# An RWKV-7 scan's tokens to token-major form by two transpositions and two full products, one sums' corner in another bank, thirteen low parts on GpSimd

## The chip, the cores and the metric

The kernel runs on one core of one Trainium2 chip. The metric is the time of one execution in device microseconds; lower is better. One execution of the kernel before was also taken by the hardware profiler, and all rows below are of that one. PE is the matmul engine (TensorE) and PEld its weight load, DVE is VectorE, ACT ScalarE, POOL GpSimd, SP the engine that issues the DMAs.

## The reference

A hybrid decoder of two layers over 272 tokens (16 learned meta tokens and 256 inputs) of width 2048: layer 0 mixes by RWKV-7, layer 1 by stick-breaking attention, each followed by a SwiGLU network. The change touches layer 0's mixing alone, whose core is a scan with 32 heads of 64:

```python
kk = heads(k * k_k)
kk = kk * lax.rsqrt(jnp.maximum(jnp.sum(kk * kk, axis=-1, keepdims=True), 1e-24))
k = k * (1.0 + (a - 1.0) * k_a)
def step(state, inp):
    r_t, d_t, k_t, v_t, kk_t, a_t = inp
    sa = jnp.einsum('bhvk,bhk->bhv', state, -kk_t)
    state = (state * d_t[:, :, None, :]
             + sa[..., None] * (kk_t * a_t)[:, :, None, :]
             + v_t[..., None] * k_t[:, :, None, :])
    return state, jnp.einsum('bhvk,bhk->bhv', state, r_t)
...
mean = jnp.mean(y, axis=-1, keepdims=True)
var = jnp.mean(jnp.square(y - mean), axis=-1, keepdims=True)
y = ((y - mean) * lax.rsqrt(var + GN_EPS)).reshape(b, l, d) * gn_w + gn_b
bonus = (jnp.sum(rh * kh * r_k, axis=-1, keepdims=True) * vh).reshape(b, l, d)
out = ((y + bonus).astype(h.dtype) * g) @ w_o
```

## The kernel before

**Numbers and layout.** Activations lie with the feature on the partitions and the token on the free axis. A product of full precision is three matmuls of a short float form: high part by high part, low by high, high by low (`mm3k`, L205 to L207). A high part is a cast on ACT, the low part what DVE subtracts (`whl_pair`, L233 and L234, for weights; `parts`, L1218 and L1219, and `split` for activations).

**The scan.** `scan` runs over 16 pairs of heads, one pair to 128 partitions, in a pipeline of several pairs: in round n, pair A = n makes its states and outputs, M = n + 1 the inverse of its triangular blocks, B = n + 2 its scores, and C = n + 3 its decays and keys. Rounds 0 to 12 are steady and come from `period`, which lists the work in the order in which PE executes it; the rounds before and after have an order of their own. Between the pieces, `f(k)` takes k steps from a stream: each step is the three matmuls of one block of 128 rows of the V or R projection of a coming pair, and the stream also splits the weights, a 128x512 piece to every four steps, several pieces ahead of use.

**Order.** PE's order and SP's are as written. On DVE, ACT and POOL the framework's scheduler places the instructions, by what they need and when it thinks that this comes; a few are tied by hand. An engine executes its instructions in order.

**Pieces that the change touches.**
- The eight PSUM banks are given out in steady rounds by `PLAN` (L50): the names in one bank's string take turns in it, and each waits until the one before was read. `ba` and `bb` hold the scores of the two heads, `b00` and `b01` the blocks of `neg` (L1380, one per head), `rm0` and `rm1` the transition products (L1524), `z0` the scores of the 16 meta tokens (L1300), `cb` the states and outputs of pair A.
- `lora` makes a pair's decay (`ld`, `L`, `P`, `Q`) from `zw`, the iclr `ta` from `za`, and keys: `AR0` and `ARV` (scaled queries, keys and values; four chunks by three kinds by 64 tokens), `B0` and `BK` (two kinds). `after_v` and `after_r` fill in the values and queries as the projections come out.
- `turned` and `tokens` bring the chunks into token-major form: `tb` by transposition, `tv` by products with an identity (`ident`, keys) and a centering matrix (`cen`, values), 64 tokens each, four each, and `X` takes both from one 128x512 copy. `values` adds the products `kv`, two copies into `X`; `apply` (L1506) multiplies by the inverse `Tt` and copies the results `Ah` and, into `X`, the states' input.
- The block inverses: `scores` masks `sb` into `G` on DVE (L1351), a DMA brings the blocks to `As`, `solve` on POOL inverts the 16x16 blocks (L1402, L1404), `inverse` brings them back as `Tt` by DMA (L1411, L1414), and `left` and `right` (`yb` L1476, `Ys`, `zb` L1495) double the block size.
- Group norm: `A.sq` is y squared (L1569); `parts` splits it into `hs`; `norm` multiplies `hs` by a block of ones (`vb`, L1213 as in `bonus`) and finishes on ACT and DVE. In `period` the split stands behind `C.lora()`, then come eight stream steps, then `norm`.
- The output projection: the stream's last steps split the pairs' outputs `o` (L953, `split`, DVE at L277) and multiply them. `KHEAD` = 13 outputs are used by the first four blocks.

Of the kernel before, what the change touches and what calls it, by code (L numbers as in the profile page):

```python
# [49 lines left out]
PLAN = {name: bank for bank, names in {  # L50
    "pfr0": "zb32 b00 z0v bonus gp", "pfr1": "wa yb16 zw kv", "psc0": "ba b01 zb16 za",
    "psc1": "bb rm0 tv vb", "psd0": "cb yb32", "psd1": "z0 rm1 tb k0"}.items()
    for name in names.split()}
# [5 lines left out]
ASTEP = 4  # L59
BUFS = {n: 2 for n in "BK AR0 G An Tt X BV0".split()}  # L60
BUFS.update(ARV=3, bv=3, pe=4)

# [75 lines left out]
class Builder:  # L138
# [132 lines left out]

    def split(self, src, pool):

        nc = self.nc
        x = self.pair_tile(pool, src.shape[1])
        nc.scalar.copy(x[0], src)
        nc.vector.tensor_tensor(x[1], src, x[0].bitcast(F32), ALU.subtract)  # L277
        return x
# [103 lines left out]
    def time_mix(self):  # L382
# [15 lines left out]
        with ExitStack() as ctx:  # L398
# [3 lines left out]
            self.s2 = []  # L402
            zero = sp.tile([128, 4, 2, 2, 64], F32, name="zero", tag="X", bufs=BUFS["X"])
            zero = zero.rearrange("p a b c t -> p (a b c t)")[:, :325]
# [381 lines left out]
    def period(self, n, A, M, B, C, D, f):  # L786

        M.inverse()
        if n > 0:
            A.right(32)  # L790
        A.start()
        B.scores(0)
        B.scores(1)
        if n > 0:
            A.apply()
        B.chunk0()
        B.chunk0_out()
# [12 lines left out]
        M.right(16)  # L810
        A.step(4)
        B.tokens(A.copied)
        B.bonus()
        C.lora()
        A.squares = A.parts(A.sq)
        f(8)
        A.norm()
        f(8)
        M.left(32)
        B.values()  # L820
        f(4)
# [103 lines left out]
    def stream(self, pairs):  # L925
# [22 lines left out]
        for m, k in steps:  # L948
# [3 lines left out]
            while len(self.o) <= k:  # L952
                self.o.append(self.split(self.oraw[len(self.o)], self.xs1))  # L953
            self.mm3k(self.wo[m], next(w), self.o[k], k == 0, False)
# [232 lines left out]
class Pair:  # L1187
# [34 lines left out]
    def lora(self):  # L1222
# [34 lines left out]

        self.ARV = ARV = self.big("ARV", 4, 3, 64)
        self.BK = BK = self.big("BK", 4, 2, 64)
# [8 lines left out]
        def par(tile, first, second):  # L1268
# [4 lines left out]
        V.scalar_tensor_tensor(AR0[:, 0], kk[:, :META], -1.0, P[:, :META], ALU.mult, ALU.mult)  # L1273
        V.scalar_tensor_tensor(ARV[:, :, 1], kk[:, META:].rearrange("p (c t) -> p c t", t=C), -1.0,
                               Pc[:, :, :C], ALU.mult, ALU.mult)
# [6 lines left out]
    def after_v(self, vp):  # L1282
        A = self.A
        A.copy(self.V0[:, 32:32 + META], vp[:, :META])
        A.copy(self.ARV[:, :, 2], vp[:, META:].rearrange("p (c t) -> p c t", t=C))

    def after_r(self, rp):
        V = self.V
        V.tensor_tensor(self.AR0[:, 1], rp[:, :META], self.P[:, 1:17], ALU.mult)
        V.tensor_tensor(self.ARV[:, :, 0], rp[:, META:].rearrange("p (c t) -> p c t", t=C),  # L1290
                        self.Pc[:, :, 1:], ALU.mult)
# [3 lines left out]

    def chunk0(self):

        z0 = self.b.rbank("z0")
        for h in HS:
            self.PE.matmul(z0[h, 0:32], self.B0[h], self.AR0[h].rearrange("p s t -> p (s t)"),  # L1300
                           start=True, stop=True)
        self.z0 = z0
# [29 lines left out]
    def scores(self, i):  # L1332
# [4 lines left out]
        for c, h in ORDER[4 * i:4 * i + 4]:  # L1337
            u = (c - 1) * 128
            for s in range(2):
                self.PE.matmul(self.sb[h][HS[s], u:u + 128], self.BK[HS[h], c - 1, s],  # L1340
                               self.ARV[HS[h], c - 1, 0:2].rearrange("p s t -> p (s t)"),
                               start=True, stop=True)
# [32 lines left out]
    def neg(self):  # L1375
        b = self.b
        b0 = [b.rbank("b00"), b.rbank("b01")]
        for c, h in ORDER:
            q, r = (c - 1) // 2, (c - 1) % 2
            self.PE.matmul(b0[h][HS[r], q * 64:(q + 1) * 64], self.ARV[HS[h], c - 1, 1],  # L1380
                           self.BK[HS[h], c - 1, r], start=True, stop=True)
# [4 lines left out]
    def bonus(self):  # L1386
        bp = self.head_sums("bonus", self.b.blk[0], self.rk, 0)
        self.bv = self.t272("bv")
        self.V.tensor_tensor(self.bv[:, :META], self.V0[:, 32:32 + META], bp[:, :META], ALU.mult)
        c4 = lambda x: x[:, META:].rearrange("p (c t) -> p c t", t=C)  # L1390
        self.b.last = self.V.tensor_tensor(c4(self.bv), self.ARV[:, :, 2], c4(bp), ALU.mult)

# [33 lines left out]
    def tokens(self, after=None):  # L1426
# [5 lines left out]
        tv = b.rbank("tv", 1)  # L1432
        for r in range(2):
            for q in range(2):
                u = (r * 2 + q) * 128
                c = q * 2 + r
                PE.matmul(tv[HS[r], u:u + 128], self.ARV[:, c, 1], b.cst("ident"), start=True, stop=True)
                PE.matmul(tv[HS[1 - r], u:u + 128], self.ARV[:, c, 2], b.cst("cen"), start=True, stop=True)
        for r in range(2):
            with b.tc.issue_after(after.ins) if after else nullcontext():  # L1440
                A.copy(self.G0[:, :, :, r],
                       tb[:, r * 256:r * 256 + 256].rearrange("p (q h t) -> p h q t", q=2, h=2))
        self.X = X = self.big("X", 4, 2, 2, 64)
        A.copy(X[:, :, 0], tv.rearrange("p (c h t) -> p c h t", c=4, h=2))

    def values(self):
# [4 lines left out]
        for h in range(2):  # L1451
            for c in range(1, 5):
                q, r = (c - 1) // 2, (c - 1) % 2
                PE.matmul(kv[HS[r], (h * 2 + q) * 64:(h * 2 + q + 1) * 64],
                          self.G2[HS[1 - r], h, q, r], X[HS[1 - r], r * 2 + q, 0, h],
                          start=True, stop=True)
        for h in HS:
            PE.matmul(k0[h, 0:64], self.SC0[h, 0:64], self.BV0[h, 64:128], start=True, stop=True)
        for r in range(2):
            A.copy(X[HS[r], r * 2:r * 2 + 2, 1],  # L1460
                   kv[HS[r], 0:256].rearrange("p (h q t) -> p q h t", q=2, h=2))
        self.KV0 = self.big("KV0", 64)
# [36 lines left out]
    def apply(self):  # L1499
# [3 lines left out]
        for h in range(2):  # L1503
            for c in range(1, 5):
                q, r = (c - 1) // 2, (c - 1) % 2
                self.PE.matmul(wa[HS[r], (h * 2 + q) * 128:(h * 2 + q + 1) * 128],  # L1506
                               self.Tt[HS[r], h * 2 + q], X[HS[r], r * 2 + q, :, h],
                               start=True, stop=True)
# [4 lines left out]
        for r in range(2):  # L1513
            b.latest = self.A.copy(X[HS[r], r * 2:r * 2 + 2, 0], wa4[HS[r], :, :, 1])

    def trans(self):
# [9 lines left out]
        for r in range(2):  # L1526
# [3 lines left out]
            b.last = V.tensor_tensor(self.Rh.rearrange("p (q r) t -> p q r t", q=2)[:, :, r], x[:, :, 1],  # L1530
                            self.ARV.rearrange("p (q r) s t -> p q r s t", q=2)[:, :, r, 0], ALU.add)

# [116 lines left out]
```

## Time and profile before

| | |
|---|---|
| median of 3 runs | 2640.32 us (2638.05 to 2641.45) |
| the profiled execution's own time | 2635.57 us |
| its span | 2633.8 us |
| instructions | 54589 |
| scan, from the first weights' steps to the last | about 165 to 600 us of the span |
| a steady round | 24.54 us |
| granted TensorE clock | 1.00 |

The profiled execution lasts 1.8 us longer than its span, and 4.75 us less than the median of the runs. Starts in the rows are us from the start of the span. Sums of row lengths are no PE time: matmuls overlap, so what counts is the distance from start to start. In rows of waits the name behind the arrow is what came last.

### The profile page before, as it was taken

The page shows a single profiled execution, that of the slowest core. Times are in us where ns is not written, and L with a number is a line of the kernel's source. Part 1 is how long each engine was busy: PE and PEld are TensorE (multiplying, and loading weights), DVE is VectorE, ACT ScalarE, POOL GpSimd, SP SyncE. Part 2 cuts the span into 40 slices and gives each one's busy share as a digit, 9 for nine tenths or more (in the row PEclk, how much of TensorE's full clock was granted, in tenths as well). Part 3 has the DMA queues.
Part 4 walks back from the last instruction along what each step waited for, and adds up shares of the span by engine and source line. Part 5 has one row for each costly group of instructions (what it writes and reads, how often), then busy time and mean ns, then how long its engine had stood idle before and what let it go on. Part 6 is the DMA issues. An engine that isn't in the chain of part 4 may idle for free.

```text
span 2633.8 us, 54589 instructions
## 1 busy us (share of the span) xinstructions
PE 2614.5 (99%) x21238; PEld 2448.2 (93%) x21238; DVE 1787.7 (68%) x3606; ACT 1496.0 (57%) x3049; POOL 182.4 (7%) x493
## 2 busy tenths in 40 slices
PE   9999999999999999999999999999999999999999
PEld 8898999889999999999999999998888888888888
DVE  7677777857555555555558775788766666666665
ACT  7776666756544444444446664786555454554553
POOL 0014445430000000000000000000000000000000
PEclk9999999999999999999999999999999999999999
DMA  6444445445555655655655555434565665665655
GB/s 228 147 122 131 119 112 130 110 131 186 171 171 173 182 171 173 184 171 169 184 171 172 178 169 176 144 113 150 184 190 179 196 190 176 200 186 180 199 181 176
DMA packets 186388, 439.45 MB, mean 167 GB/s; under 512 B 58736, under 2 KB 89616, under 8 KB 186128
## 3 DMA queue, kind: packets, MB, share of 16 engines
q1 hardware_dynamic: 184784, 432.77, 53.3%
q8 instruction: 166, 2.72, 0.4%
q0 software_dynamic: 768, 2.23, 0.3%
q10 hardware_dynamic: 576, 0.96, 0.1%
q14 instruction: 94, 0.77, 0.1%
HBM read 430.15 MB, written 5.74 MB: 165 GB/s over the span
## 4 chain that ended last, share of the span: by engine, by line
PE 96%; DVE 2%; ACT 1%; DMA 1%; POOL 0%; issue 0%; SPq 0%; ACTq 0%; POOLq 0%
PE mm L210 23%; PE mm L205 17%; PE mm L207 17%; PE mm L206 17%; PE mm L209 12%; PE lr L607 1%; PE mm L508 1%; PE cb L1561 1%; DVE G L1351 1%; PE zb L1495 1%; PE z L1145 1%; PE yb L1476 1%; PE cb L1553 0%; DMA Tt<-s 0%; PE ba L1340 0%; PE hms L1060 0%
## 5 line engine op out<-in xcount | busy, mean ns | idle before, releaser
L187 DVE TENSOR_TENSOR wlo<-raw,whi 128x512 fp32r<-128x512 f32 (+1 forms) x1432 | 967.7, 679 | 597.9 <-ACT whi L186 577.8
L186 ACT CAST whi<-raw 128x512 fp32r<-128x512 f32 (+1 forms) x1432 | 870.9, 610 | 837.1 <-PE mm L206 530.5
L205 PE MATMUL mm<-hl,whi 128*128 128x272 f32 x3328 | 961.8, 289 | 0.0
L207 PE MATMUL mm<-hl,wlo 128*128 128x272 f32 x3328 | 960.4, 289 | 0.0
L206 PE MATMUL mm<-hl,whi 128*128 128x272 f32 x3328 | 958.0, 288 | 0.0
L210 PE MATMUL mm<-hl,whi 128*128 128x512 f32 x2624 | 919.9, 394 | 0.0
L209 PE MATMUL mm<-hl,wlo 128*128 128x256 f32 x2624 | 738.5, 282 | 0.1
L206 PEld LDWEIGHTS mm<-hl,whi 128*128 128x128 f32 x3328 | 631.1, 190 | 0.0
L205 PEld LDWEIGHTS mm<-hl,whi 128*128 128x128 f32 x3328 | 625.4, 188 | 3.4 <-issue 1.7
L207 PEld LDWEIGHTS mm<-hl,wlo 128*128 128x128 f32 x3328 | 625.5, 188 | 0.2
L210 PEld LDWEIGHTS mm<-hl,whi 128*128 128x128 f32 x2624 | 492.6, 188 | 111.8
L209 PEld LDWEIGHTS mm<-hl,wlo 128*128 128x128 f32 x2624 | 494.4, 188 | 1.1 <-DVE ht L1067 0.4
L234 DVE TENSOR_TENSOR wlo<-raw,whi 128x512 fp32r<-128x512 f32 (+2 forms) x156 | 105.6, 690 | 20.1 <-ACT whi L233 18.0
L233 ACT CAST whi<-raw 128x512 fp32r<-128x512 f32 (+2 forms) x156 | 91.8, 608 | 23.2 <-PE mm L206 20.8
L1402 POOL TENSOR_TENSOR Tm<-As 40x14 f32<-40x14 f32 (+6 forms) x224 | 85.0, 379 | 211.2 <-DMA As<-s 169.8
L226 DVE TENSOR_TENSOR h<-h,mm 128x256 f32<-128x256 f32 (+1 forms) x224 | 93.9, 420 | 6.7 <-PE mm L210 6.0
L1404 POOL TENSOR_TENSOR As<-As,Tm 40x14 f32<-40x14 f32 (+6 forms) x224 | 86.3, 385 | 16.6
L219 ACT COPY c<-mm 128x256 f32<-128x256 f32 x104 | 38.8, 373 | 67.5 <-PE mm L210 67.5
L205 PE MATMUL mm<-hi,whi 128*128 128x272 f32 x256 | 75.5, 295 | 0.0
L206 PE MATMUL mm<-lo,whi 128*128 128x272 f32 x256 | 73.7, 288 | 0.0
L207 PE MATMUL mm<-hi,wlo 128*128 128x272 f32 x256 | 73.5, 287 | 0.0
L205 PEld LDWEIGHTS mm<-hi,whi 128*128 128x128 f32 x256 | 48.1, 188 | 1.1
(314 smaller groups left out, 2377.4 us busy)
## 6 DMA issues: line engine op xcount, KB each, us to landing
raw<-w_gate SPq DMA_DIRECT2D x176, 512.0 KB
raw<-w_up SPq DMA_DIRECT2D x176, 512.0 KB
raw<-w_down SPq DMA_DIRECT2D x128, 512.0 KB
raw<-w_down SPq DMA_DIRECT2D x128, 192.0 KB
raw<-w_v SPq DMA_DIRECT2D x32, 512.0 KB
raw<-w_r SPq DMA_DIRECT2D x32, 512.0 KB
raw<-sb_w_k SPq DMA_DIRECT2D x32, 512.0 KB
raw<-sb_w_v SPq DMA_DIRECT2D x32, 512.0 KB
```

The lines of the kernel that those rows point to most:

```text
L186: nc.scalar.copy(hi, part)
L187: nc.vector.tensor_tensor(lo, part, hi.bitcast(F32), ALU.subtract)
L205: mm(out, w[0], x[0], start=first, stop=False)
L206: mm(out, w[0], x[1], start=False, stop=False)
L207: return mm(out, w[1], x[0], start=False, stop=last)
L209: mm(out[:, :n], w[1], x[0], start=first, stop=False, skip_group_check=True)
L210: return mm(out, w[0], x[2], start=False, stop=last, skip_group_check=True)
L226: self.nc.vector.tensor_tensor(h, h, out[:, c:c + n], ALU.add)
L233: self.cast = nc.scalar.copy(hi, part)
L234: self.rest = nc.vector.tensor_tensor(lo, part, hi.bitcast(F32), ALU.subtract)
L1402: V.tensor_tensor(t, As[:, 0:i, i:i + 1].to_broadcast([40, i, n]), As[:, i:i + 1, i + 1:].to_broadcast([40, i, n]), ALU.mult)
L1404: V.tensor_tensor(As[:, 0:i, i + 1:], As[:, 0:i, i + 1:], t, ALU.add)
```

## The change

Five edits are made in the scan.
- `tokens`: the two chunks 2q and 2q + 1 stand side by side, so one transposition of 128 columns takes two chunks of keys and one product with `cen` two of values. For this `ARV` is laid out kind first (three by four by 64), and the values are written with the chunks of each couple exchanged (`swapped`). Keys and `kv` go to a new tile `AK`, values to a half as large `X`; the copies are split accordingly, and `values` has one copy where it had two.
- `PLAN`: `b01` and `rm1` change banks, and `z0` has none: in steady rounds it is written into columns 464 to 495 of `cb`, without clearing.
- `split` may take another engine; the low parts of the first 13 outputs go to GpSimd.
- Round 0: three of the eight stream steps ahead of `A.norm` go ahead of `A.start`.
- The zeroed tile at the start is half as large, as `X` is.

```diff
-    "pfr0": "zb32 b00 z0v bonus gp", "pfr1": "wa yb16 zw kv", "psc0": "ba b01 zb16 za",
-    "psc1": "bb rm0 tv vb", "psd0": "cb yb32", "psd1": "z0 rm1 tb k0"}.items()
+    "pfr0": "zb32 b00 z0v bonus gp", "pfr1": "wa yb16 zw kv", "psc0": "ba rm1 zb16 za",
+    "psc1": "bb rm0 tv vb", "psd0": "cb yb32", "psd1": "b01 tb k0"}.items()
...
-BUFS = {n: 2 for n in "BK AR0 G An Tt X BV0".split()}
+BUFS = {n: 2 for n in "BK AR0 G An Tt X AK BV0".split()}
...
-    def split(self, src, pool):
+    def split(self, src, pool, engine=None):
...
-        nc.vector.tensor_tensor(x[1], src, x[0].bitcast(F32), ALU.subtract)
+        (engine or nc.vector).tensor_tensor(x[1], src, x[0].bitcast(F32), ALU.subtract)
...
         if n > 0:
             A.right(32)
+        else:
+            f(3)
         A.start()
...
-        B.chunk0()
+        B.chunk0(A.cb)
...
         A.squares = A.parts(A.sq)
-        f(8)
+        f(8 if n > 0 else 5)
         A.norm()
...
-                self.o.append(self.split(self.oraw[len(self.o)], self.xs1))
+                self.o.append(self.split(self.oraw[len(self.o)], self.xs1,
+                                         self.nc.gpsimd if len(self.o) < KHEAD else None))
...
-        self.ARV = ARV = self.big("ARV", 4, 3, 64)
+        self.ARV = ARV = self.big("ARV", 3, 4, 64)
...
-        A.copy(self.ARV[:, :, 2], vp[:, META:].rearrange("p (c t) -> p c t", t=C))
+        A.copy(self.swapped(), vp[:, META:].rearrange("p (q r t) -> p q r t", q=2, r=2))
+
+    def swapped(self):
+
+
+        return self.ARV[:, 2].rearrange("p (q r) t -> p q r t", q=2)[:, :, ::-1]
...
-    def chunk0(self):
-
-        z0 = self.b.rbank("z0")
+    def chunk0(self, cb=None):
+
+        z0 = cb[:, T + 192:T + 224] if self.b.steady else self.b.rbank("z0")
         for h in HS:
             self.PE.matmul(z0[h, 0:32], self.B0[h], self.AR0[h].rearrange("p s t -> p (s t)"),
-                           start=True, stop=True)
+                           start=not self.b.steady, stop=True, skip_group_check=True)
...
-        for r in range(2):
-            for q in range(2):
-                u = (r * 2 + q) * 128
-                c = q * 2 + r
-                PE.matmul(tv[HS[r], u:u + 128], self.ARV[:, c, 1], b.cst("ident"), start=True, stop=True)
-                PE.matmul(tv[HS[1 - r], u:u + 128], self.ARV[:, c, 2], b.cst("cen"), start=True, stop=True)
+        for q in range(2):
+            PE.transpose(tv[:, q * 128:q * 128 + 128], self.ARV[:, 1, q * 2:q * 2 + 2].rearrange("p c t -> p (c t)"), b.cst("ident"))
+        for q in range(2):
+            PE.matmul(tv[:, 256 + q * 128:384 + q * 128], self.ARV[:, 2, q * 2:q * 2 + 2].rearrange("p c t -> p (c t)"), b.cst("cen"),
+                      start=True, stop=True)
...
-        self.X = X = self.big("X", 4, 2, 2, 64)
-        A.copy(X[:, :, 0], tv.rearrange("p (c h t) -> p c h t", c=4, h=2))
+        self.AK = self.big("AK", 2, 2, 2, 64)
+        A.copy(self.AK[:, :, 0], tv[:, :256].rearrange("p (q h t) -> p q h t", q=2, h=2))
+        self.X = X = self.big("X", 2, 2, 2, 64)
+        for r in range(2):
+            A.copy(X[HS[1 - r], r], tv[HS[1 - r], 256:].rearrange("p (q h t) -> p q h t", q=2, h=2))
...
-        for r in range(2):
-            A.copy(X[HS[r], r * 2:r * 2 + 2, 1],
-                   kv[HS[r], 0:256].rearrange("p (h q t) -> p q h t", q=2, h=2))
+        A.copy(self.AK[:, :, 1], kv[:, 0:256].rearrange("p (h q t) -> p q h t", q=2, h=2))
...
-                               self.Tt[HS[r], h * 2 + q], X[HS[r], r * 2 + q, :, h],
+                               self.Tt[HS[r], h * 2 + q], self.AK[HS[r], q, :, h],
...
-            b.latest = self.A.copy(X[HS[r], r * 2:r * 2 + 2, 0], wa4[HS[r], :, :, 1])
+            b.latest = self.A.copy(X[HS[r], r], wa4[HS[r], :, :, 1])
...
-                    x = self.X[:, r * 2 + q, 0, i]
+                    x = self.X[:, r, q, i]
```

What is left out of the diff follows from `ARV`'s new layout: the same elements under other indices.

The scheduler places DVE's and ACT's work differently behind these edits, in each of the thirteen steady rounds alike. DVE, a middle round, from the transposition `Tn` of pair M on; `hs` is the low part of A's squares, `ld` to `BK` are C's decays and keys, `wlo` the low part of stream weights. Before:

```order
L1472 STREAM_TRANSPOSE Tn<-Tt 128x256
L1219 TENSOR_TENSOR hs<-sq,hs 128x272
L1235 TENSOR_SCALAR ld<-ld 128x272
L1236 SCALAR_TENSOR_TENSOR L<-consts,ld 128x272
L1249 TENSOR_SCALAR k_6469<-ta,vecs,dv 128x272
L1253 SCALAR_TENSOR_TENSOR kk<-kt,vecs,rn 128x272
L1250 TENSOR_TENSOR k_6469<-k_6469,kt 128x272
L1273 SCALAR_TENSOR_TENSOR AR_6476<-kk,P 128x16
L1274 SCALAR_TENSOR_TENSOR ARV<-kk,P 128x4x64
L234 TENSOR_TENSOR wlo<-raw,whi 128x512
L1276 SCALAR_TENSOR_TENSOR kk<-ta,kk 128x272
L1279 TENSOR_TENSOR B_0_2035<-k_6469,Q 128x16
```

The same place now:

```order
L1480 STREAM_TRANSPOSE Tn<-Tt 128x256
L1238 TENSOR_SCALAR ld<-ld 128x272
L1239 SCALAR_TENSOR_TENSOR L<-consts,ld 128x272
L1252 TENSOR_SCALAR k_6442<-ta,vecs,dv 128x272
L1256 SCALAR_TENSOR_TENSOR kk<-kt,vecs,rn 128x272
L1253 TENSOR_TENSOR k_6442<-k_6442,kt 128x272
L1276 SCALAR_TENSOR_TENSOR AR_6449<-kk,P 128x16
L1277 SCALAR_TENSOR_TENSOR ARV<-kk,P 128x256
L1282 TENSOR_TENSOR B_0_2035<-k_6442,Q 128x16
L1283 TENSOR_TENSOR BK<-k_6442,Q 128x2x128
L1279 SCALAR_TENSOR_TENSOR kk<-ta,kk 128x272
L1222 TENSOR_TENSOR hs<-sq,hs 128x272
```

`hs` moved from ahead of `ld` to behind the second `kk`, ten instructions later; `wlo` moved out of this stretch to behind it.

ACT in the same round, from the square of A's output on; `X<-tv` is the copy of `tokens`, `V` and `ARV<-mm` are the values of a pair, `whi` the high part of stream weights. Before:

```order
L1569 ACTIVATE sq<-y 128x272
L1444 COPY X<-tv 128x4x128
L1218 CAST hs<-sq 128x272
L1234 ACTIVATE ld<-zw,dv 128x272
L1238 ACTIVATE ta<-za,dv 128x272
L1284 COPY V_0_2037<-mm 128x16
L1285 COPY ARV<-mm 128x4x64
L233 CAST whi<-raw 128x512
L1241 ACTIVATE P<-L 128x16
```

Now:

```order
L1577 ACTIVATE sq<-y 128x272
L1451 COPY AK<-tv 128x2x128
L1454 COPY X<-tv 64x256 x2
L1237 ACTIVATE ld<-zw,dv 128x272
L1241 ACTIVATE ta<-za,dv 128x272
L1221 CAST hs<-sq 128x272
L1287 COPY V_0_2037<-mm 128x16
L1288 COPY ARV<-mm 128x2x2x64
L1244 ACTIVATE P<-L 128x16
```

The cast `hs`, the high part of the squares, moved behind `ld` and `ta`, and the cast `whi` went from ahead of `P` to a place behind `Q`.

PE keeps its order; the matmuls of `tokens`, between the last outputs `cb` and `bonus`, are now these (before, eight `tv` of 64x128, keys and values in turn):

```order
L1569 MATMUL cb<-Rh,S 64x64 x2
L1442 MATMUL tv<-consts,ARV 128x128 x2
L1444 MATMUL tv<-consts,ARV 128x128 x2
L1216 MATMUL bonus<-hs,blk 128x272 x2
L205 MATMUL zw<-dec_w1h,w2h 128x272
```

Four `tv` of twice the stationary columns stand where eight stood, and nothing else moved around them.

More of the change, by code (lines that the diff above doesn't have):

```diff
@@ L402, in time_mix @@
             self.s2 = []
-            zero = sp.tile([128, 4, 2, 2, 64], F32, name="zero", tag="X", bufs=BUFS["X"])
+            zero = sp.tile([128, 2, 2, 2, 64], F32, name="zero", tag="X", bufs=BUFS["X"])
             zero = zero.rearrange("p a b c t -> p (a b c t)")[:, :325]
@@ L1273, in lora @@
         V.scalar_tensor_tensor(AR0[:, 0], kk[:, :META], -1.0, P[:, :META], ALU.mult, ALU.mult)
-        V.scalar_tensor_tensor(ARV[:, :, 1], kk[:, META:].rearrange("p (c t) -> p c t", t=C), -1.0,
+        V.scalar_tensor_tensor(ARV[:, 1], kk[:, META:].rearrange("p (c t) -> p c t", t=C), -1.0,
                                Pc[:, :, :C], ALU.mult, ALU.mult)
@@ L1289, in after_r @@
         V.tensor_tensor(self.AR0[:, 1], rp[:, :META], self.P[:, 1:17], ALU.mult)
-        V.tensor_tensor(self.ARV[:, :, 0], rp[:, META:].rearrange("p (c t) -> p c t", t=C),
+        V.tensor_tensor(self.ARV[:, 0], rp[:, META:].rearrange("p (c t) -> p c t", t=C),
                         self.Pc[:, :, 1:], ALU.mult)
@@ L1340, in scores @@
                 self.PE.matmul(self.sb[h][HS[s], u:u + 128], self.BK[HS[h], c - 1, s],
-                               self.ARV[HS[h], c - 1, 0:2].rearrange("p s t -> p (s t)"),
+                               self.ARV[HS[h], 0:2, c - 1],
                                start=True, stop=True)
@@ L1379, in neg @@
             q, r = (c - 1) // 2, (c - 1) % 2
-            self.PE.matmul(b0[h][HS[r], q * 64:(q + 1) * 64], self.ARV[HS[h], c - 1, 1],
+            self.PE.matmul(b0[h][HS[r], q * 64:(q + 1) * 64], self.ARV[HS[h], 1, c - 1],
                            self.BK[HS[h], c - 1, r], start=True, stop=True)
@@ L1389, in bonus @@
         self.V.tensor_tensor(self.bv[:, :META], self.V0[:, 32:32 + META], bp[:, :META], ALU.mult)
-        c4 = lambda x: x[:, META:].rearrange("p (c t) -> p c t", t=C)
-        self.b.last = self.V.tensor_tensor(c4(self.bv), self.ARV[:, :, 2], c4(bp), ALU.mult)
+        c4 = lambda x: x[:, META:].rearrange("p (q r t) -> p q r t", q=2, r=2)
+        self.b.last = self.V.tensor_tensor(c4(self.bv), self.swapped(), c4(bp), ALU.mult)
     def solve(self):
@@ L1454, in values @@
                 PE.matmul(kv[HS[r], (h * 2 + q) * 64:(h * 2 + q + 1) * 64],
-                          self.G2[HS[1 - r], h, q, r], X[HS[1 - r], r * 2 + q, 0, h],
+                          self.G2[HS[1 - r], h, q, r], X[HS[1 - r], r, q, h],
                           start=True, stop=True)
@@ L1530, in trans @@
             b.last = V.tensor_tensor(self.Rh.rearrange("p (q r) t -> p q r t", q=2)[:, :, r], x[:, :, 1],
-                            self.ARV.rearrange("p (q r) s t -> p q r s t", q=2)[:, :, r, 0], ALU.add)
+                            self.ARV[:, 0].rearrange("p (q r) t -> p q r t", q=2)[:, :, r], ALU.add)
     def half(self, kind, c, i):
```

## The prediction

> **What bounds the kernel now.** I read the head of the page first, then the waits of TensorE inside the scan, then the span cut at equal places of two neighbouring periods.
>
> ```profile
> span 2633.8 us, 54589 instructions
> PE 2614.5 (99%) x21238; PEld 2448.2 (93%) x21238; DVE 1787.7 (68%) x3606; ACT 1496.0 (57%) x3049; POOL 182.4 (7%) x493
> PE 96%; DVE 2%; ACT 1%; DMA 1%; POOL 0%; issue 0%; SPq 0%; ACTq 0%; POOLq 0%
> ```
>
> The first line is the span, the second the busy time of each engine, the third the share of each engine in the chain that ended last. PE is busy 99% and makes 96% of the chain. So a change counts by what it takes from PE's stream and by what it makes PE wait; time saved on VectorE (DVE), ScalarE (ACT) or GpSimd (POOL) alone is worth nothing.
>
> Of the waits of PE between 165 and 602 us (what waits, for what; us in total, times, longest) these touch the change:
>
> ```profile
> PE b L1380 <- DVE G L1351: 4.9, 13, 1.2
> PE zb L1495 <- DVE o L1592: 2.7, 2, 1.7
> PE yb L1476 <- DMA Tt<-s: 1.9, 3, 1.2
> PE wa L1506 <- DVE Tt L1496: 1.0, 1, 1.0
> ```
>
> They sum to 10.5 us: the most that the removal of every one could bring. The table of windows, cut where the second triangular product `zb` begins, gives one of the steady periods:
>
> ```profile
> 361.03:385.57 24.54, 24.25 (x378) 22.95 (x377) 18.96 (x48) 16.77 (x41) 11.14 (x29) 1.00 0.41 120
> ```
>
> The columns are the stretch, its length, then busy time and count of PE, PEld, DVE, ACT and POOL, the granted clock (1.00) and the DMA share. PE has 0.29 us free in 24.54, so every period is at its limit by PE, and what a period gains or loses is told by PE's row of starts.
>
> **Tokens.** PE's timeline (start, length, count) has the products `tv` as 16 records in 8 pairs, of which these are the first and the last:
>
> ```profile
> 369.11 0.32 PE L1437 MATMUL tv<-consts,ARV 128*64 128x128 f32 x1
> ...
> 369.93 0.27 PE L1437 MATMUL tv<-consts,ARV 128*64 128x128 f32 x1
> ```
>
> The two of a pair begin together (two halves of the array), so 7 pairs take 369.93 − 369.11 = 0.82 us, 0.11 to 0.12 a pair, 0.109 behind the first. Eight matmuls leave 16 records, two each. Two transposes of one record and two full products of two make 6 records in a row: two slots less, **−0.22 us a period**. Were the transposes two records as well, it would be nothing; I take −0.22.
>
> **Banks.** `rm1` and `b01` change places, and `z0` goes into the bank of `cb`.
>
> ```profile
> 363.50 0.30 PE L1380 MATMUL b<-BK,ARV 64*64 64x64 f32 x2
> 364.08 0.38 PE L1380 MATMUL b<-BK,ARV 64*64 64x64 f32 x9 [0.28 <-DVE G L1351]
> 364.26 0.27 PE L1524 MATMUL rm<-G,Ah 64*64 64x128 f32 x1
> 364.27 0.29 PE L1380 MATMUL b<-BK,ARV 64*64 64x64 f32 x5
> 364.37 0.66 PE L1524 MATMUL rm<-G,Ah 64*64 64x128 f32 x15
> 364.96 0.34 PE L1553 MATMUL cb<-X,G 128*64 128x64 f32 x4
> ```
>
> `b01` shares a bank with `ba`, which the first masked copy `G` must have read. PE idles 0.28 us for it, and between the first two starts of `b` lie 0.58. Behind the change that wait is gone, but `rm1` now stands in the bank of `ba`, and two more answers come just as late:
>
> ```profile
> 363.35 0.68 DVE L1351 TENSOR_TENSOR G<-ba,consts 128x512 f32<-128x512 f32 x1
> 363.62 0.37 ACT L1512 COPY Ah<-wa 128x256 f32<-128x256 f32 x1 [1.95 <-PE wa L1506]
> 363.89 0.76 ACT L1514 COPY X<-wa 64x256 f32<-64x256 f32 x2
> ```
>
> `G` is done at 364.03, so `rm1` is free when `b` is through. `rm` reads `Ah`, done at 363.99; `cb` reads `X`, done at 364.65. `cb` can therefore begin at 364.65 plus a semaphore's way (0.05: G's 364.03 to PE's 364.08), some 364.70 for 364.96. I take **−0.24**; nothing if `rm` only waits where `b` did, −0.5 if the copies of `X` come as much earlier as `b` does.
>
> **The sums for the norm.** This is the term that decides. `A.squares` splits the squared outputs into a high part (ACT) and a low part (DVE); `vb` on PE multiplies both, eight steps of the projections behind `za`. PE's order there is left alone, but the order listings show that in every steady period DVE's low part `hs` now stands behind the decay chain of the next pair, and ACT's cast behind `ld` and `ta`. Before:
>
> ```profile
> 374.13 0.28 PE L207 MATMUL mm<-hi,wlo 128*128 128x272 f32 x1
> 374.26 0.41 PE L1213 MATMUL vb<-hs,blk 128*128 128x272 f32 x2
> ```
>
> ```profile
> 371.47 0.43 DVE L1219 TENSOR_TENSOR hs<-sq,hs 128x272 fp32r<-128x272 f32 x1
> 371.82 0.31 DVE L1235 TENSOR_SCALAR ld<-ld 128x272 f32<-128x272 f32 x1
> ...
> 374.72 0.77 DVE L234 TENSOR_TENSOR wlo<-raw,whi 128x512 fp32r<-128x512 f32 x1
> 375.41 0.52 DVE L1276 SCALAR_TENSOR_TENSOR kk<-ta,kk 128x272 f32<-128x272 f32 x1
> 375.85 0.26 DVE L1279 TENSOR_TENSOR B<-k,Q 128x16 f32<-128x16 f32 x1
> ...
> 376.37 0.26 DVE L1277 TENSOR_TENSOR B<-kk,Q 128x16 f32<-128x16 f32 x1
> ```
>
> ```profile
> 370.25 0.58 ACT L1444 COPY X<-tv 128x512 f32<-128x512 f32 x1 [0.18 <-PE tv L1438]
> 370.75 0.42 ACT L1218 CAST hs<-sq 128x272 fp32r<-128x272 f32 x1
> 371.07 0.48 ACT L1234 ACTIVATE ld<-zw,dv 128x272 f32<-128x272 f32 x1
> ...
> 373.29 0.63 ACT L233 CAST whi<-raw 128x512 fp32r<-128x512 f32 x1
> 373.81 0.23 ACT L1241 ACTIVATE P<-L 128x16 f32<-128x16 f32 x1
> ```
>
> Now the low part is ready at 371.90, 2.4 us ahead of its use. After the change:
> - ACT: `X` and the cast took 0.50 + 0.32 ahead of `ld`. The new copies are one of 128x256 (as `Ah`, 0.27 from start to start) and two of 64x256 (0.76 together); the first can begin 0.22 earlier. `ld` starts at 371.0 to 371.1, as it did.
> - DVE's `ld` starts when ACT's is done, 371.05 + 0.48, and no longer behind `hs`: 371.55 for 371.82, −0.27.
> - At `kk` (375.41) the `wlo` of 0.69 is no longer ahead, but `B` and `BK` are (375.85 to 376.37, 0.52). `P` begins up to 0.52 earlier, since the cast `whi` moves behind it; what DVE waited for it is at most 0.3. `kk` starts at 375.41 − 0.69 + 0.52 − 0.27 − (0 to 0.3) = 374.67 to 374.97, `hs` 0.44 later, and ends 0.43 behind that: 375.54 to 375.84.
> - PE wants it for the second `vb` at 374.26 + 0.13 − 0.22 = 374.17.
>
> That is a stall of 1.37 to 1.67 and a semaphore's 0.05. I take **+1.45**, near the lower end, because the cast ahead of `P` surely goes; bounds 1.2 (all of the chain's gains larger) and 1.95 (none of them). Queued behind PE's waiting `vb` is the next `f(8)`, eight projection steps that are ready but stand behind it; DVE and ACT do the weight splits that were moved meanwhile, so I count no second wait for those.
>
> One rule bears on it, and no number below uses this. Of the starts quoted above, an `rm` (364.26) stands ahead of a `b` (364.27) that is ahead of it in the program. The Trainium skill, "TensorE: Matmul & The Clock Gate", Part 3 (the mechanism of packing small matmuls), says that matmuls start and end in program order, with no reordering. The trace agrees where it counts here: between 363.50 and 364.08 nothing passes the waiting `b`; the two starts 0.01 apart speak for records of different quarters of the array rather than for a queue that looks ahead. By the rule the whole stall stands; if PE could take ready steps from behind `vb`, it would be zero, which is the first rival's sum.
>
> **Low parts on GpSimd.** Twelve low parts of `o` leave DVE near n = 12.
>
> ```profile
> 508.41 2.54 DVE L277 TENSOR_TENSOR hl<-o,hl 128x272 fp32r<-128x272 f32 x7
> 508.74 0.68 PE L1495 MATMUL zb<-Ys,Tn 64*64 64x64 f32 x16
> 511.43 1.09 PE L1506 MATMUL wa<-X,Tt 64*64 64x128 f32 x16 [1.02 <-DVE Tt L1496]
> 514.65 0.34 PE L1553 MATMUL cb<-X,G 128*64 128x64 f32 x4
> 534.81 0.39 PE L1495 MATMUL zb<-Ys,Tn 64*64 64x64 f32 x6 [1.73 <-DVE o L1592]
> ```
>
> From `zb` to `cb` this period takes 514.65 − 508.74 = 5.91 us, the other one 364.96 − 361.03 = 3.93: the seven low parts of 508.41 delay `Tt` and then `G`. Without them most of these 2.0 go, between 1.0 (the wait for `Tt` alone) and 2.0; I take **−1.8**, the bank gain in it. The stall at `vb` falls away in this period, since PE waits 1.73 for `o` at its end anyway. On GpSimd,
>
> ```profile
> 371.39 0.20 POOL L1402 TENSOR_TENSOR Tm<-As 40x14 f32<-40x14 f32 x1 [11.77 <-DMA As<-s]
> ...
> 378.11 0.29 POOL L1402 TENSOR_TENSOR Tm<-As 40x56 f32<-40x56 f32 x1
> ```
>
> 42 elements more cost 0.09 us, so 272 come to about 0.75 by estimate; twelve take 9 us behind the solve that ends near 508, done by 520, ahead of the output projection's first use near 535. At twice the price they would end by 526, still ahead of it.
>
> **Period 0.** Three steps move ahead of `A.start`; there
>
> ```profile
> 217.91 0.88 PE L1476 MATMUL yb<-Tt,An 64*64 64x64 f32 x15 [1.17 <-DMA Tt<-s]
> ```
>
> PE waits 1.17 us for `Tt`, whose landing is set by GpSimd, not by PE. Nine matmuls of 0.13 (374.13 to 374.26) fill it, so they are free. But `vb` then stands five steps behind `za`, not eight, and waits 1.13 longer. So −0.22 − 1.13 + (1.45 + 1.13) = **+1.2**; the bank gain is lost in the wait.
>
> **The sum**, against the profiled execution of 2635.57 us (span 2633.8 and 1.8 around it): periods 1 to 11 give 11 × (−0.22 − 0.24 + 1.45) = +10.9; the other two waits of `yb` (1.9 − 1.2 = 0.7) are covered by longer periods, −0.7; period 0 +1.2; period 12 −1.8; two tokens outside the steady periods −0.4. Together +9.2 us. The median of the three runs, 2640.32, stands 4.75 above the profiled execution; carried over it gives 2649.5. Cost at nothing: the new copies `AK`, `X`, `swapped` and the mask of `z0` on ACT and DVE, which move as many elements as before beside PE's 24.25 busy us, and the DMAs, whose order on SP's queue is the same row for row. If the copies took twice as long, `ld` would start 0.6 later and the stall would be 2.0, which is the worse case below.
>
> **The rivals.**
> - *Faster: PE isn't held at `vb`.* If DVE's chain reaches `kk` by 373.3, 1.4 us sooner than I make it (or ready steps pass `vb`), the stall is nothing. Then 11 × −0.46 − 0.7 − 0.2 − 1.8 − 0.4 = −8.2: 2632. For it speaks that DVE is busy only 18.96 of 24.54; against it, that each link from `ld` to `hs` waits for the one before.
> - *About the same: half the stall.* With 0.8 a period, 11 × 0.34 + 0.6 − 0.7 − 1.8 − 0.4 = +1.4: 2642. It needs `kk` 0.65 sooner than my range; `P` would have to bring twice the 0.3.
> - *Worse: the bank change doesn't do what it says.* `rm` waits for `Ah` and `ba` as `b` did, and the stall is 1.9: 11 × (1.9 − 0.22) + 1.7 − 0.7 − 1.8 − 0.4 = +17.3: 2658. For it: `Ah` is done only 0.04 ahead of `G`.
>
> **How the numbers follow.** Chances: forecast 0.50, worse 0.22, same 0.18, faster 0.10. A measurement can tell about 0.2% (5.3 us) from no change; +9.2 and +17 lie above, +1.4 within, −8.2 below. The range of 2640 to 2658 takes in the half stall and the worse case and leaves out the faster one and a tail above.
>
> **What would show it.** In the changed profile: PE's `vb` waits for DVE `hs` in thirteen periods, 1.2 to 1.9 us each; period length about 25.5; 6 `tv` records, 0.2 us less; no `b<-G` wait, and `cb` not over 3.7 behind `zb`; the first `yb` still at the landing of `Tt`; `zb` to `cb` of n = 12 about 4. I am wrong if `hs` ends before 374.2 on this scale, or if another wait (weights split late, `Tt` landing) follows `vb`.

## The result and the profile after

The changed kernel took 2657.0 us (median of 4 runs, 2651.1 to 2659.4) beside 2639.5 for the kernel before (2638.1 to 2641.5): ratio 1.0068, 95% interval 1.0056 to 1.0080. It is slower by 17.5 us. The forecast was 2649.5, slower, in a range of 2640 to 2658. When the changed kernel was run again, one more execution took 3612.1 us at a mean granted clock of 0.65; it is in none of the figures here.

The profiled execution was the shortest of the four (2651.07 us, span 2649.3). The head of its page:

```profile
span 2649.3 us, 54383 instructions
PE 2612.1 (99%) x21078; PEld 2446.0 (92%) x21078; DVE 1788.5 (68%) x3593; ACT 1499.3 (57%) x3065; POOL 188.6 (7%) x506
PE 94%; DVE 2%; ACT 2%; issue 1%; DMA 1%; POOL 0%; SPq 0%; POOLq 0%
```

PE is busy 2.4 us less, its share of the chain is 94% for 96%, and the span is 15.5 us longer: PE waits, or runs slower. The longest waits of PE in the scan (what, for what; total, times, longest):

```profile
PE vb L1216 <- DVE hs L1222: 21.6, 13, 2.8
PE yb L1484 <- DMA Tt<-s: 2.1, 2, 1.6
PE zb L1503 <- DVE o L1600: 1.8, 2, 0.9
PE zb L1503 <- DVE Ys L1489: 1.7, 2, 1.4
PE rm L1532 <- DVE G L1359: 0.6, 2, 0.4
```

The 4.9 us of `b` for `G` are gone, and 21.6 us of `vb` for `hs` have come, once in each of the thirteen steady rounds. One such place, on PE and then on DVE (start, length, engine, line):

```profile
352.75 0.44 PE L1442 MATMUL tv<-consts,ARV 128*128 128x128 f32 x2
353.02 0.61 PE L1444 MATMUL tv<-consts,ARV 128*128 128x128 f32 x4
353.39 0.50 PE L1216 MATMUL bonus<-hs,blk 128*128 128x272 f32 x2
...
357.48 0.28 PE L1216 MATMUL vb<-hs,blk 128*128 128x272 f32 x1
359.50 0.39 PE L1216 MATMUL vb<-hs,blk 128*128 128x272 f32 x1 [1.73 <-DVE hs L1222]
```

```profile
355.22 0.36 DVE L1238 TENSOR_SCALAR ld<-ld 128x272 f32<-128x272 f32 x1 [0.44 <-ACT ld L1237]
...
358.48 0.52 DVE L1279 SCALAR_TENSOR_TENSOR kk<-ta,kk 128x272 f32<-128x272 f32 x1
358.92 0.52 DVE L1222 TENSOR_TENSOR hs<-sq,hs 128x272 fp32r<-128x272 f32 x1
```

PE does the first product of `vb` at 357.48 and stands until DVE, through with the decay chain, makes the low part (358.92 + 0.52). The tokens take six records and 0.64 us to `bonus` (353.39 − 352.75) where they took 1.02. The same round, cut at the same place as before:

```profile
344.93:370.78 25.85, 24.03 (x367) 22.67 (x367) 19.30 (x48) 16.97 (x43) 10.35 (x29) 1.00 0.44 117
```

It lasts 25.85 for 24.54, with PE 0.22 busy less. One thing wasn't foreseen. Behind the longest wait, in round 0, the granted clock (the number ahead of the last two) falls to half:

```profile
228.00:230.00 2.00, 0.65 (x5) 0.65 (x6) 2.00 (x7) 1.74 (x3) 1.64 (x5) 1.00 0.33 80
230.00:232.00 2.00, 2.00 (x11) 2.00 (x11) 1.21 (x2) 0.37 (x2) 1.73 (x4) 0.52 0.26 78
232.00:234.00 2.00, 2.00 (x13) 2.00 (x11) 0.69 (x1) 1.97 (x3) 1.54 (x6) 0.63 0.63 239
234.00:236.00 2.00, 2.00 (x49) 1.78 (x48) 1.67 (x5) 1.46 (x5) 0.22 (x1) 1.00 0.83 232
```

### The profile page after: what moved, and what is told of

Its sections match the earlier page's. It is cut to its first block, busy times and chain, and to the rows that moved or that the text cites. A ratio compares the mean times of both kernels' runs of the same rounds, so it can differ in the third digit from the quotient of the medians.

```text
span 2649.3 us, 54383 instructions
## 1 busy us (share of the span) xinstructions
PE 2612.1 (99%) x21078; PEld 2446.0 (92%) x21078; DVE 1788.5 (68%) x3593; ACT 1499.3 (57%) x3065; POOL 188.6 (7%) x506
## 4 chain that ended last, share of the span: by engine, by line
PE 94%; DVE 2%; ACT 2%; issue 1%; DMA 1%; POOL 0%; SPq 0%; POOLq 0%
PE mm L210 23%; PE mm L205 16%; PE mm L207 16%; PE mm L206 16%; PE mm L209 12%; PE lr L607 1%; PE mm L508 1%; PE cb L1569 1%; PE z L1148 1%; PE yb L1484 1%; PE wa L1514 1%; PE cb L1561 1%; PE ba L1348 0%; PE zb L1503 0%; PE rm L1532 0%
```

## The experiments

Each ran against the kernel before on the same chip; ratios are to that, with 95% intervals.

**The order on DVE and ACT, undone.** In the changed kernel `parts` is called ahead of `lora`, and `ld` on ACT and DVE is tied behind the two halves of the split; both engines then have the order of the kernel before.

```diff
+        A.squares = A.parts(A.sq)
+        self.low_sums = A.split
         C.lora()
-        A.squares = A.parts(A.sq)
+        self.low_sums = None
...
+        self.split = hi, lo
...
+        if b.low_sums:
...
+            for x, y in zip((th, de), b.low_sums):
+                b.tc.add_manual_dep(x.ins, y.ins.name, nosync, reason="sums first")
```

> The changed kernel, with the split of the squares put back ahead of ld on ACT and DVE, as it stands in the kernel before; nothing else differs. My theory (PE stalls at vb because hs comes late): the 21.6 us of waits at vb are gone; a steady round falls from about 25.7 us to 23.9 to 24.4, the rest being what a wait for Tt takes back; the time is about 2633 us (2629 to 2638), under the 2639 of the kernel before. Rival (the loss sits in the new products, copies or banks themselves): rounds stay over 25 us and the time over 2648.

Measured: 2633.6 us, ratio 0.9984 (0.9972 to 0.9996). The three longest entries among PE's waits:

```profile
PE yb L1491 <- DMA Tt<-s: 5.8, 6, 2.0
PE zb L1510 <- DVE Ys L1496: 2.8, 2, 2.5
PE zb L1510 <- DVE o L1607: 2.3, 2, 1.4
```

No `vb` is among them. Undisturbed rounds last 23.87 us. So the order carries the loss; without it the change gains, and the next limit is the landing of `Tt`, on which PE now waits six times instead of three. The scheduler put `wlo` and `whi` back together with `hs`, here and, the other way, in the next experiment; that it is `hs` and not they is read from the waits, which name `hs`.

**The order alone.** In the kernel before, the two halves of the split are tied behind `ta` on ACT and the second `kk` on DVE (`C.chain`).

```diff
-        A.squares = A.parts(A.sq)
+        A.squares = A.parts(A.sq, C.chain)
...
+            for p, q in zip((hi, lo), behind):
+                self.b.tc.add_manual_dep(p.ins, q.ins.name, nosync, reason="sums late")
```

> The kernel before, with the split of the squares tied behind ta on ACT and behind the second kk on DVE, which gives those engines the order of the changed kernel; PE, the banks and the products are those of before. My theory: the order alone makes a stall at vb of 1.1 to 1.3 us in each steady round (PE is there 0.6 later than in the changed kernel), rounds of about 25.7 us, and a time of about 2652 us (2648 to 2656). Rival (the order costs nothing): 2639.

Measured: 2654.9 us, ratio 1.0059 (1.0044 to 1.0074). The two longest entries:

```profile
PE vb L1213 <- DVE hs L1219: 16.4, 13, 1.4
PE b L1384 <- DVE G L1355: 4.8, 13, 1.2
```

Nothing of the change is in this kernel but the order, and it makes 16.8 of the 17.5 us. Here `vb` is reached later than in the changed kernel, so each wait is some 0.3 us shorter (1.25 for 1.57, the means of rounds 1 to 12), and the other edits' gains are missing.

**Four more steps ahead of `vb`** in the changed kernel, order left as it is.

```diff
-        f(8 if n > 0 else 5)
+        f(12 if n > 0 else 9)
         A.norm()
-        f(8)
+        f(4)
```

> The changed kernel, with four of the eight stream steps behind A.norm moved ahead of it; DVE and ACT keep their late hs. My theory: 12 matmuls of 0.125 (1.5 us) fill the stall of about 1.75, some 0.2 of it is left, and the time is about 2634 us (2630 to 2641). Rival (DVE or ACT sets the pace of the round, not PE's wait at this place): the wait moves along with vb and the time stays over 2650.

Measured: 2639.9 us, ratio 1.0006 (0.9996 to 1.0015); `vb` waits 1.7 us in all. The stall is filled, which rules out that DVE or ACT paces the round; but it is no more than the kernel before. Later `vb` makes `o` later: PE waits up to 2.5 us for `Tt`, 2.5 for `Ys` and 1.8 for `o`, and behind each of these stands half clock.

**The banks alone**, in the kernel before.

```diff
-    "pfr0": "zb32 b00 z0v bonus gp", "pfr1": "wa yb16 zw kv", "psc0": "ba b01 zb16 za",
-    "psc1": "bb rm0 tv vb", "psd0": "cb yb32", "psd1": "z0 rm1 tb k0"}.items()
+    "pfr0": "zb32 b00 z0v bonus gp", "pfr1": "wa yb16 zw kv", "psc0": "ba rm1 zb16 za",
+    "psc1": "bb rm0 tv vb", "psd0": "cb yb32", "psd1": "b01 tb k0"}.items()
...
-        z0 = self.b.rbank("z0")
+        z0 = cb[:, T + 192:T + 224] if self.b.steady else self.b.rbank("z0")
```

> The kernel before with the banks alone: b01 and rm1 change places, z0 in cb's bank. My theory: -0.27 us a round up to the first yb, no wait of b for G; some of it taken back by yb waiting for Tt; the time is 2636 to 2639. Rival (rm waits where b did): the wait stands at rm with 0.2 us or more, and the time is that of the kernel before, 2639.5.

Measured: 2635.6 us beside 2638.1, ratio 0.9990 (0.9980 to 1.0001): a gain about as large as the steady rounds show (24.27 for 24.54, 0.27 each), though the interval just reaches no change. `rm` waits 0.6 us in round 0 and 1.1 in round 12, and in the rounds between not at all.

**The tokens alone**, in the kernel before, with the split kept ahead of `ld` (`ARV`, `AK`, `X`, `swapped` and the four products as in the change).

> The kernel before with the new tokens alone (ARV, AK, X and their copies), and the split of the squares kept ahead of ld. My theory: the products save 0.35 to 0.4 us a steady round, of which yb's wait for Tt takes some back; rounds of 24.15 to 24.4 us and a time of 2633 to 2637 us beside 2638 for the kernel before. Rival (the new copies on ACT make something late): rounds of 24.5 us or more, 2638 or more.

Measured: 2633.6 us beside 2637.4, ratio 0.9980 (0.9970 to 0.9990). Rounds of 24.13 for 24.54: 0.41 us each.

**GpSimd's low parts alone**, in the kernel before (the edit of `split` and its call).

> The kernel before with the low parts of 13 outputs on GpSimd alone. Theory of the prediction (they cost nothing there): the wait of wa for Tt (1.0 us) and of b for G in round 12 goes, nothing comes instead, 2636.3 us beside 2638.1. Rival, from the profile of the changed kernel (a DVE operation on SBUF alone, w2l, lasts 2.6 us and ends when GpSimd's twelve end): w2l of round 12 lasts over 2 us here too, zb waits for Ys over 1 us, and the gain is eaten: 2637.5 to 2641.

Measured: 2640.1 us, ratio 1.0011 (1.0002 to 1.0020): a little slower, not faster. The profile is of the shortest of the eleven runs (2635.7 us). `wa` no longer waits, but in the round ahead `zb` waits 1.9 us for `o`. On DVE and on POOL at that place:

```profile
504.54 3.26 DVE L1584 SCALAR_TENSOR_TENSOR y<-y,dv,bv 128x272 f32<-128x272 f32 x1
```

```profile
504.55 2.95 POOL L277 TENSOR_TENSOR hl<-o,hl 128x272 fp32r<-128x272 f32 x4
```

An operation of 0.5 us (0.50 in the same kernel's other rounds) lasts 3.26 and ends 0.3 after GpSimd's row of four. It is `y`, not `w2l`: the rival named the wrong instruction, but an instruction of DVE held beside GpSimd's row, and the eaten gain, came as it said.

**Round 0 undone**, in the changed kernel (eight steps ahead of `norm`, none ahead of `A.start`).

> The changed kernel without the edit of round 0 (no three steps ahead of A.start, eight ahead of A.norm). Theory (a long wait of PE is followed by 3.4 us at half clock): the wait at vb of round 0 is 1.7 instead of 2.84 us and no half clock follows it, the wait at yb is 1.2 to 1.6; round 0, rm to rm, takes 28 to 29.5 us instead of 31.3, and the time is 2 to 3 us under that of the changed kernel, about 2654. Rival (the length of a wait doesn't matter for the clock): round 0 is 0.1 to 0.3 longer than with the edit, since three steps more stand ahead of the same end.

Measured: 2652.3 us, ratio 1.0054 (1.0040 to 1.0067), against 1.0068 with the edit: about 3.7 us less, though the intervals overlap. The profile is of the longest of the four runs (2655.8 us). From `rm` to `rm`, round 0 lasts 28.4 us, its `vb` waits 1.76, and no half clock follows that. But at its start stands a wait of 2.39 us, where the changed kernel waits 0.57 (what, for what; total, times, longest):

```profile
PE rm L1530 <- DVE G L1357: 2.4, 1, 2.4
```

`G` stands on DVE behind weight splits for which ACT waited 2.74 us for a DMA (0.62 to 1.05 in the profiles before, after and of a typical run), and half clock lies behind that wait, from 215.67 to 219.08. So `rm` of round 1 begins at 243.81, beside 245.19 in the changed kernel's first profile and 243.78 in the typical one below. These profiles bear out what the wait at `vb` costs, not that the edit's removal gains the 3.7 us; whether the late DMA has to do with the edit is not shown.

**Split ahead, low parts on DVE**: the changed kernel without its GpSimd edit and with the first experiment's order.

> The changed kernel with the split of the squares ahead of ld and the low parts of the outputs on DVE as before. Theory (GpSimd's low parts hold DVE up in round 12): the wait of zb for Ys of 2.5 us and the half clock behind it are gone, wa waits 1.0 for Tt instead; the time is 2630 to 2632 us, 1 to 3 under that of the run with the split ahead alone (2633.6). Rival (GpSimd takes nothing): 2635, 1.8 over it.

Measured: 2633.6 us, ratio 0.9982 (0.9973 to 0.9992): the same as with GpSimd, and neither the 2630 to 2632 of the theory nor the 2635 of the rival. DVE's own low parts cost about what GpSimd's hold costs in that setting (there `w2l` lasts 4.36 us beside GpSimd's row of twelve); the experiment doesn't tell the two apart.

**Low parts on DVE, `hs` late**: the changed kernel without its GpSimd edit.

> The changed kernel with the low parts of the outputs back on DVE; hs stays late. Theory (GpSimd's run of low parts holds DVE for as long as it lasts, more or less of it from run to run): the time is 2650 to 2653 us beside 2657 of the changed kernel, the runs lie closer together than its 2651 to 2659, zb's wait for Ys in round 12 is under 0.4. Rival (the prediction's term, the low parts cost 1.8 on DVE and nothing on GpSimd): 2658 to 2659.

Measured: 2653.8 us (2653.2 to 2654.6), ratio 1.0054 (1.0041 to 1.0066). The runs lie within 1.4 us where the changed kernel's lie within 8, and the median is some 3 us lower, a little above the 2650 to 2653 expected; the intervals overlap. So it is likely, though not shown by the times alone, that GpSimd's low parts cost in the changed kernel. The small spread holds only where `hs` is late (0.4 us in the kernel with the order alone): with `hs` ahead the runs spread over 9.3 us with the low parts on DVE too (2627.9 to 2637.3 in the experiment before this one).

**The changed kernel again**, for a profile of a typical run.

> The changed kernel once more, for a second profile: the first one was of its shortest run (2651.1 beside 2656.7 to 2659.4). Theory (the longer runs are those in which GpSimd's back-to-back low parts hold a DVE operation longer): if this profile is of a run over 2655, a DVE operation around rounds 11 and 12 lasts 4 to 9 us and PE waits 3 us or more for what follows it; the runs spread over 6 us or more, wider than the 1.4 us with the low parts on DVE. Rival (the longer runs have late landings of Tt, or more half clock elsewhere): no DVE operation over 3 us there, and the extra time stands at yb.

Measured: ratio 1.0068 (1.0055 to 1.0081), runs of 2649.3 to 2659.3. This profile is of a run of 2656.98. On DVE, POOL and PE at the end of round 11, and the windows there:

```profile
521.12 8.38 DVE L1222 TENSOR_TENSOR hs<-rs,hs 128x272 fp32r<-128x272 f32 x1
529.42 0.48 DVE L1600 SCALAR_TENSOR_TENSOR o<-y,vecs,gp 128x272 f32<-128x272 f32 x1
```

```profile
521.24 7.96 POOL L277 TENSOR_TENSOR hl<-o,hl 128x272 fp32r<-128x272 f32 x11
```

```profile
529.96 1.12 PE L1503 MATMUL zb<-Ys,Tn 64*64 64x64 f32 x16 [6.25 <-DVE o L1600]
```

```profile
527.00:529.00 2.00, 0.00 (x0) 0.00 (x0) 2.00 (x1) 0.00 (x0) 2.00 (x4) 0.83 0.00 0
529.00:531.00 2.00, 1.04 (x22) 1.04 (x26) 0.91 (x2) 0.42 (x1) 0.71 (x2) 0.50 0.00 0
531.00:533.00 2.00, 2.00 (x40) 2.00 (x38) 0.42 (x1) 0.00 (x0) 0.27 (x1) 0.50 0.03 8
533.00:535.00 2.00, 2.00 (x32) 2.00 (x34) 1.38 (x3) 0.25 (x1) 0.00 (x0) 0.50 0.00 0
```

The split of `rk` for the bonus, an operation of some 0.47 us, begins 0.12 ahead of GpSimd's row of eleven and ends 0.3 behind it. `o` stands behind it on DVE, PE waits 6.25 us for `o`, and runs at half clock for some 5 us more. The profile with round 0 undone has the same: 8.39 us beside 7.96, and a wait of 6.30. In the first profile GpSimd's row fell later and met another operation near its end:

```profile
529.58 2.63 DVE L860 TENSOR_TENSOR w2l<-w,w2h 128x512 fp32r<-128x512 f32 x1
```

The wait behind that one was 1.4 us (`zb` for `Ys`), without half clock. Rounds 11 and 12 make 7.1 of the 5.9 us by which the two profiles differ, round 0 takes 1.5 back.

**Each low part twice**, on the first experiment's kernel.

```diff
-        (engine or nc.vector).tensor_tensor(x[1], src, x[0].bitcast(F32), ALU.subtract)
+        for _ in range(2 if engine else 1):
+            (engine or nc.vector).tensor_tensor(x[1], src, x[0].bitcast(F32), ALU.subtract)
```

> The changed kernel with the split of the squares ahead of ld (2633.6), and each of the 13 low parts on GpSimd made twice in a row. It measures whether the run on GpSimd holds DVE. Theory (a DVE operation with all operands in SBUF doesn't proceed until GpSimd's row of low parts is through): one DVE operation of that stretch lasts until GpSimd's row ends, 10 to 17 us, PE waits for it by 8 us or more longer, and the time is 2642 to 2650. Rival (the long DVE operation there was a coincidence, or each waits its turn): no DVE operation over 5 us, and a time of 2633 to 2637.

Measured: 2641.9 us, ratio 1.0002 (0.9992 to 1.0012), at the lower edge of the theory's 2642 to 2650. But its mechanism missed: no DVE operation is held to the end of the row. DVE and POOL there, and from the list of PE's waits:

```profile
519.03 0.85 DVE L1242 TENSOR_SCALAR ld<-ld 128x272 f32<-128x272 f32 x1
519.92 1.24 DVE L1247 TENSOR_TENSOR_SCAN L<-consts,ld 128x272 f32<-128x272 f32 x1
```

```profile
507.92 22.77 POOL L278 TENSOR_TENSOR hl<-o,hl 128x272 fp32r<-128x272 f32 x24
```

```profile
PE zb L1511 <- DVE o L1608: 7.4, 2, 6.6
```

Most of DVE's operations on SBUF from `ld` on are some 0.5 us longer (`ld` 0.85 for 0.36, the scan 1.24 for 0.73), though `ARV` and `BK` keep their 0.41; GpSimd's are 0.95 each (22.77 / 24) for the 0.72 of the row of eleven. They seem to take turns. The delays add up along DVE's chain to `o`, for which PE waits 6.62 us, with 6.8 us at half clock. That the row costs DVE is shown; when it holds one operation to its end and when they take turns stays open.

**A version that beats both**: split ahead, low parts on DVE, and in round 12 two stream steps from behind `M.trans` to ahead of `M.right(32)`.

```diff
+        f(2)
         M.right(32)
         f(2)
         M.apply()
         f(2)
         M.trans()
-        f(2)
```

> The changed kernel with the split of the squares ahead of ld, the low parts on DVE, and in round 12 the last two stream steps moved from behind M.trans to ahead of M.right(32), where PE waits 1.9 us for o. Theory (two steps, 0.75 us, fit into that wait, and a wait of 1.2 is not followed by half clock): the wait is 1.2, no half clock near 530 us, and the time is 1 to 2.5 us under 2633.6, so 2631 to 2632.5. Rival (M.trans's results are then waited for, or the half clock comes anyway): 2633.6 or more.

Measured: 2627.6 us (2626.9 to 2635.2) beside 2639.3, ratio 0.9961 (0.9947 to 0.9974). The wait is as expected:

```profile
534.53 0.68 PE L1509 MATMUL zb<-Ys,Tn 64*64 64x64 f32 x16 [1.05 <-DVE o L1606]
```

Without the edit it was 1.92 with 3.4 us at half clock behind it; here the clock stays at 1.00. The gain over the kernel without it, 0.21% by the ratios, is more than the 1 to 2.5 us expected, and the intervals touch: three of the five runs lie at 2627, two at 2633 and 2635, and the profile is of the former of these two.

## Why the prediction was right, and where its sum was not

The sign, the place and the mechanism of the main term held: PE stands at `vb` in all thirteen steady rounds, because the scheduler put DVE's `hs` behind the decay chain. The size did not: the sum, +9.2 us, was made against the profiled execution, and came out at +15.5 in the first profile (2651.07 − 2635.57) and +21.4 in the typical one (2656.98). That the median of 2657.0 still lies within the range is in part luck. It stands 1 us under the upper end, beside the 2658 of the worse rival, of which one condition came (a loss of 1.6 to 1.9 at `vb`) and the other, the lost bank gain, did not; most of the rest came from the two terms that failed, told below. By its terms, as differences between the starts of `rm` in PE's timelines, from one round to the next:

| term | predicted | first profile | typical run |
|---|---|---|---|
| before the first `rm` and from that of round 13 on | −0.4 | −1.4 | −1.2 |
| round 0 | +1.2 | +5.2 | +3.7 |
| rounds 1 to 10 | +9.2 | +10.9 | +11.0 |
| rounds 11 and 12, with GpSimd | −0.8 | +0.8 | +7.9 |

- **Tokens.** Forecast −0.22 a round by two slots; measured −0.38 in the changed kernel, −0.41 alone. The count of six records was right, the step from `tv` to `bonus` shrank by more than two slots of 0.109.
- **Banks.** Forecast −0.24; `cb` stands 3.66 behind `zb` (348.59 − 344.93) for 3.93, −0.27, and −0.27 a round alone. In rounds 1 to 11 the rival that `rm` waits where `b` did is out; in round 0 it waits 0.57 in the changed kernel, where `b` waited 1.16.
- **The stall.** Forecast 1.45, bounds 1.2 to 1.95; the waits in rounds 1 to 11 read 1.48 to 1.73. DVE's `hs` ended where it was put, 13.0 us behind the round's `wa` (359.44 and 346.44; forecast 13.0 to 13.3). PE was there 0.46 sooner than reckoned (357.48 + 0.13 is 11.17 behind `wa`, 374.17 was 11.63 behind it): by the tokens, and by the bank gain, which the forecast counted but left out of the time at which PE wants `hs`. What PE gains ahead of a wait that DVE ends makes the wait longer. PE also loses more than the wait reads: its two products of `vb` start 2.02 apart (357.48, 359.50) instead of 0.13, so 1.89 for a wait of 1.73. 1.89 − 0.38 − 0.27 = 1.24 is about what this round is longer (1.31), where the forecast had 0.99. The stall was right in kind; with a mean wait of 1.56 in rounds 1 to 11 and the same 0.16 on top it was some 0.27 a round too small, of which the tokens took back 0.16. Of the 0.18 by which rounds 1 to 10 are longer than forecast (1.17 for 0.99), 0.1 is left that these rows do not explain.
- **FIFO of PE.** The whole stall stood in every round, and no stream step from behind `vb` began before it: as the Trainium skill has it in "TensorE: Matmul & The Clock Gate", Part 3, and against the first rival.
- **Round 0: the failed step.** "So −0.22 − 1.13 + (1.45 + 1.13) = +1.2" priced a wait of 2.6 us as 2.6 us. It was 2.84, and the half clock behind it made 24 matmuls last 4.62 us instead of 3.10 (from 229.58 to `yb` at 234.20; before, 226.47 to 229.57). The wait of 1.60 at `yb` had half clock behind it too; the three steps did not shorten it (1.17 before), since PE came there sooner, with 0.57 of waits at `rm` for the 1.16 of `b`. With the edit undone, `vb` waits 1.76 in round 0 and the clock stays at 1.00 behind that wait; that profile's half clock in round 0 belongs to another wait, of 2.39 at `rm`.
- **Low parts on GpSimd: the other failed step.** "At twice the price they would end by 526" is true (8.75 us for the row of twelve, 0.73 each, about as estimated; the row ends at 531.67 in a profile that runs 13.9 us later there) and beside the point: the step looked for who waits for the low parts, not for what they take from DVE. In place of −0.8 for the two rounds, the −1.8 included, the profiles show +0.8 and +7.9, where the changed kernel with the low parts on DVE shows +0.3; the edit alone took 2.6 us more. The Trainium skill, "SBUF — State Buffer", Who interferes with whom, says that a DVE instruction with two SBUF inputs contends with a GpSimd instruction that reads SBUF, through a shared port that one of them locks. The traces agree as to who contends: what stretched furthest (`hs`, `w2l`, `y`) reads SBUF alone, while the masks `G` with an input in PSUM kept their 0.68 beside the row of twelve. But the page has the lock end with the instruction, and here one operation of DVE stood for a row of eleven. Nor do the two inputs settle every row: beside the low parts made twice, `ld` with one SBUF input was 0.5 us longer, and `ARV` and `BK` with two were not.
- **What the spread hid.** I carried the sum from the profiled execution to the median by 4.75 us. For the changed kernel that step is a matter of chance: its runs lie 8 us apart, and the two profiles differ mainly by what GpSimd's row met.

## What to carry to other kernels

When an edit adds or drops an instruction, compare the order that the scheduler makes on every engine, and look there for a product whose input has slid behind a long chain: the order of one split was worth 0.84% here (ratios 1.0068 and 0.9984, some 22 us), more than all five edits. Price a wait of PE of about 2 us or more with the slow clock behind it. Work moved to GpSimd is not free for DVE, even where nobody waits for its result.

## What the runs showed of the hardware

**Half clock behind a wait.** In the 14 profiles all fourteen waits of PE between 170 and 600 us that last 1.82 us or more are followed (or, the longest, already accompanied) by a granted clock of 0.50 for some 3.4 us in all, 6.8 behind the three of over 6 us. Of 52 waits of 1.3 to 1.73 us with nothing idle in the 5 us ahead one is; of five between 1.76 and 1.78, two; with other idle time close by it came from 1.15 us on, not each time, and once for 6.8 us (behind a wait of 1.75, in the kernel with the last steps earlier). So the waits at `vb` of 1.5 to 1.7 us stand just under the point at which each would cost, by estimate, up to 1.7 us more, half of the 3.4. The Trainium skill, "TensorE: Matmul & The Clock Gate", Part 1 (What's actually happening), gives the same 3.4 us as the length of a free-running window, and has the throttle come after an idle window: the length agrees, but a wait of half a window was enough.

**GpSimd against DVE.** Operations of DVE on SBUF beside a row of GpSimd's subtractions, of 0.26 to 0.73 us otherwise, took anything from 0.74 to 8.39 us where they were stretched, and ended 0.3 to 0.6 us behind the row where they were held (2.63, 3.26, 4.36 and 8.38 us); some, as `ARV` of 0.41, kept their length.
